# A two-layer decoder trunk on one core: the background inverses of a delta-rule layer paced among the v and gate projections, with the remainders of split numbers on VectorE

## The chip, the cores and the metric

The kernel runs on one core of a Trainium2 chip. The metric is device time in microseconds (us). The time before is the median of three runs. Engines are called as in the profile: PE is TensorE, DVE is VectorE, ACT is ScalarE, POOL is GpSimd, SP is SyncE, which here only issues transfers.

## What is computed

The input x is 1024 tokens by 1024 features. Layer 0 is a time-mixing layer with a matrix state for each of 16 heads, layer 1 a differential attention. After each, a gated input embedding (PLE) is added, and at the end stands one normalization. The change lies in layer 0, of which this is what matters:

```
dx = token_shift(h) - h
xm = h[:, :, None, :] + dx[:, :, None, :] * mu[:4]        # inputs of r, k, v and gate
proj = einsum('bsgd,dgc->bsgc', xm, w_in)                 # 1024 x 1024 each
r, k, v, gate = proj
...
def step(state, inp):                                     # over the 1024 tokens
    r_t, w_t, k_t, v_t, kk_t, b_t = inp
    sa = einsum('bhij,bhj->bhi', state, kk_t)
    state = state * w_t - sa[..., None] * b_t + v_t[..., None] * k_t
    y_t = einsum('bhij,bhj->bhi', state, r_t)
    return state, y_t
...
return (y * silu(gate)) @ w_out
```

All is 32-bit. A product of full precision is made of three matmuls: each operand is split into a rounded half (hi, on ACT) and the remainder (lo, one subtraction), and hi·hi, hi·lo, lo·hi are summed.

## The kernel before

The recurrence runs in 16 chunks of 64 tokens. For each chunk and head the steps inside the chunk need the inverse of a 64x64 triangular matrix, and these inverses depend only on k and b, not on the state. They are made ahead, as a background to two projections, in four quarters of four chunks.

One quarter goes so. For each of its four chunks PE makes products (`pb`), and DVE scales them into `nq`. DVE transposes the diagonal 32x32 blocks into `nb`. Then 31 elimination steps of two instructions each follow: `tm` is a product of one column of `nb` with a row of `tb`, and `tb` takes the sum; the operands have between 31 and 256 elements per partition. DVE transposes the result twice, into `ea` and into `ti`. The off-diagonal blocks come from two more groups of 64 small matmuls, `pg` and `po`, with ACT's copies `prhs` and `pairs` ahead of each; this is the merge. All 16 `ti` are needed before the core.

The stages in question follow the projections of k and r. The v projection (about 307 to 447 us) has 32 tiles, each with 24 matmuls of 128x256; ACT copies each tile to SBUF (`vst`) and SP stores it (`v_d`). The gate projection (447 to 565 us) has 16 blocks `d`, each with 24 matmuls of 128x512; ACT makes a tanh of it and DVE the gate (`ge`), which goes out to `sg_d`. Then comes the core: per chunk the chain of `xy`, `u` and `s` on PE, with `kbt`, `pm`, `prt` of the next chunk, and with the products `pps` of layer 1's embedding between them.

Weights come as raw rows (`wv10r`, `w_6r`, two buffers) and are split by `wload`; the inputs of the gate projection (`xm3`) are made by `make_half`: a multiply on ACT, a multiply-add on DVE, hi on ACT, lo on POOL or DVE. `split` puts remainders on POOL unless told otherwise:

```
def split(hi, lo, src, lo_eng=None):
    S.activation(hi, src, AF.Copy)
    (lo_eng or G).tensor_tensor(out=lo, in0=src, in1=hi.bitcast(F32), op=ALU.subtract)
```

The background is a generator, `inv_steps`; `tick` takes a step of it at two points of each v tile and four points of each gate block, and the work is written into the program there. Engines are in order each. Up to the core a scheduler may still move instructions within an engine's list; from the core loop on, `e.pin` keeps the order in which they are written. `first` holds the opening pieces of the core's first chunk (`stage1`: load, decayed, turn, mh, pr), which are written behind the inverses. `ple_load(1, ...)` loads and splits p and wp, the operands of `pps`, ahead of the core.

## Time and profile before

| | us |
|---|---|
| median of three runs | 1796.63 (1793.05 to 1798.04) |
| the profiled execution | 1792.27 |
| its span | 1790.4 |
| PE busy in the span | 1676.9 (94%) |
| DVE busy | 1272.1 (71%) |
| ACT busy | 798.9 (45%) |
| POOL busy | 609.0 (34%) |
| v projection, inverses in the background | about 307 to 447 |
| gate projection, inverses in the background | about 447 to 565 |
| core, 16 chunks | about 565 to 860 |

The profile shows one execution. Busy shares are means over stages with different limits. So a stage is read from its own window, then from the chain of waits, which is followed back from the last instruction, and from the rows of what each engine waited for. The table of the whole span says little about a stage.

### The profile page before, as it was taken

How to read it: one execution, taken by the hardware profiler on the slowest of the kernel's cores; microseconds unless marked ns; L12 is line 12 of the kernel's file. 1: busy time of each engine (PE TensorE's matmuls, PEld its weight loads, DVE VectorE, ACT ScalarE, POOL GpSimd, SP SyncE). 2: the span in 40 equal slices, each digit the busy share in tenths (PEclk: the TensorE clock that was granted, in tenths of full speed). 3: DMA queues.
4: the chain of work that ended last, by engine and by line, in shares of the span. 5: the costliest groups of instructions: out<-in, count | busy, mean ns of one | idle time of the engine just before them, and what ended most of it. 6: DMA issues, size and time to landing. Idle time of an engine off the chain costs nothing.

```text
span 1790.4 us, 31127 instructions
## 1 busy us (share of the span) xinstructions
PE 1676.9 (94%) x11768; PEld 1391.3 (78%) x11768; DVE 1272.1 (71%) x2910; ACT 798.9 (45%) x1690; POOL 609.0 (34%) x647
## 2 busy tenths in 40 slices
PE   6899999898998989999899899899999999999998
PEld 5677778887677878887678778788888888777786
DVE  7865845698994476666756657887787887856665
ACT  6567743346344443334434344444444444444332
POOL 4433634224323455656300342332423323311200
PEclk9999999998898999999899999999999999999999
DMA  7115444434216553453523210110111101521122
GB/s 261 53 54 165 140 121 104 131 99 117 82 62 192 168 172 119 131 167 113 212 101 135 93 60 7 53 49 17 54 33 30 56 9 55 188 70 34 59 95 71
DMA packets 164404, 176.03 MB, mean 98 GB/s; under 512 B 74845, under 2 KB 127837, under 8 KB 164254
## 3 DMA queue, kind: packets, MB, share of 16 engines
q1 hardware_dynamic: 161950, 169.84, 30.6%
q10 hardware_dynamic: 2304, 4.20, 0.6%
q8 instruction: 93, 1.52, 0.4%
q14 instruction: 57, 0.47, 0.1%
HBM read 124.19 MB, written 49.81 MB: 97 GB/s over the span
## 4 chain that ended last, share of the span: by engine, by line
PE 63%; DVE 25%; issue 4%; ACT 4%; POOL 3%; DMA 1%; SPq 0%; ACTq 0%; DVEq 0%; POOLq 0%
PE qkv L50 18%; PE d L50 7%; PE fg L50 5%; PE pg L50 5%; PE do L50 4%; PE sc L50 3%; DVE xmt L50 3%; PE xy L50 3%; PE av L50 3%; DVE tm L50 3%; PE op L50 3%; DVE tb L50 3%; DVE nb L50 2%; DVE ost L50 2%; PE pm L50 1%
## 5 line engine op out<-in xcount | busy, mean ns | idle before, releaser
L50 ACT ACTIVATE e<-sc,mx 128x256 f32<-128x256 f32 (+7 forms) x128 | 94.1, 739 | 110.7 <-DVE mx L50 59.7
L50 POOL TENSOR_TENSOR rp<-rp,rq 128x128 f32<-128x128 f32 x128 | 61.7, 503 | 227.8 <-DVE rq L50 173.8
L50 PE MATMUL sc<-k,q 128*128 128x512 f32 (+2 forms) x384 | 88.7, 363 | 3.8 <-ACT e L50 2.2
L50 PE MATMUL av<-vh,aT 128*128 128x128 f32 x576 | 81.2, 281 | 6.3 <-DVE aT L50 6.3
L50 PEld LDWEIGHTS av<-vh,aT 128*128 128x128 f32 x576 | 75.6, 195 | 12.8 <-DVE aT L50 8.9
L50 POOL TENSOR_TENSOR m<-m,mmask 128x512 f32<-128x512 f32 x32 | 47.9, 1496 | 81.7 <-ACT m L50 81.7
L50 DVE TENSOR_REDUCE mxs<-sc 128x1 f32<-128x128 f32 (+6 forms) x112 | 73.9, 680 | 0.5
L50 PEld LDWEIGHTS sc<-k,q 128*128 128x128 f32 x384 | 63.2, 190 | 12.9 <-ACT e L50 3.0
L50 PE MATMUL pg<-pwg,ph 128*128 128x512 f32 x224 | 73.2, 405 | 0.0
L50 PE MATMUL do<-dwo,oh 128*128 128x512 f32 x224 | 71.7, 401 | 0.8 <-DVE h L50 0.6
L50 DVE SCALAR_TENSOR_TENSOR xmt<-hT,cB,xmt 128x512 f32<-128x512 f32 x64 | 63.6, 1011 | 6.2 <-ACT xmt L50 5.8
L50 ACT ACTIVATE o<-av,r 128x128 f32<-128x128 f32 x64 | 23.5, 368 | 90.1 <-PE av L50 89.9
L50 DVE TENSOR_TENSOR tm<-tb,nb 128x31 f32<-128x31 f32 (+15 forms) x124 | 57.1, 461 | 3.6
L50 DVE SCALAR_TENSOR_TENSOR e<-e,r,e 128x128 f32<-128x128 f32 (+3 forms) x64 | 56.7, 887 | 1.2
L50 POOL CAST q<-q 64x128 fp32r<-64x128 f32 x128 | 38.8, 304 | 52.2 <-PE sc L50 48.0
L50 POOL CAST k<-k 64x256 fp32r<-64x256 f32 x64 | 25.7, 401 | 84.6 <-ACT k L50 83.5
L50 DVE TENSOR_TENSOR tb<-tb,tm 128x31 f32<-128x31 f32 (+15 forms) x124 | 51.8, 417 | 3.6
L50 DVE TENSOR_TENSOR rp<-qkv,rc 128x256 f32<-128x256 f32 x64 | 27.0, 421 | 36.7 <-PE qkv L50 34.0
L50 DVE COPY aT<-at 128x512 f32<-128x512 f32 (+2 forms) x96 | 51.8, 549 | 1.1 <-PE at L50 0.4
L50 PE MATMUL at<-ident,e 128*128 128x128 f32 x288 | 47.4, 277 | 3.1 <-DVE e L50 2.6
L50 DVE SCALAR_TENSOR_TENSOR ost<-ost 128x2 f32<-128x2 f32 x192 | 47.4, 247 | 3.8
L50 DVE TENSOR_TENSOR m<-pm,mmask 128x512 f32<-128x512 f32 x32 | 22.1, 691 | 38.2 <-PE pm L50 38.1
(1136 smaller groups left out, 5602.7 us busy)
## 6 DMA issues: line engine op xcount, KB each, us to landing
pp_d<-ppo SPq DMA_DIRECT2D x32, 256.0 KB, 2.5
kb_d<-kb SPq DMA_DIRECT2D x16, 512.0 KB, 3.3
kkr<-kkr_d SPq DMA_DIRECT2D x32, 256.0 KB, 3.8
kb<-kb_d SPq DMA_DIRECT2D x32, 256.0 KB, 3.5
x<-in_x SPq DMA_DIRECT2D x8, 512.0 KB, 5.8
kkr_d<-ep SPq DMA_DIRECT2D x16, 256.0 KB, 2.6
kkr_d<-rt SPq DMA_DIRECT2D x16, 256.0 KB, 2.6
bb<-kb_d SPq DMA_DIRECT2D x32, 128.0 KB, 2.9
```

The source lines that it names most:

```text
L50: r = f(*a, **k)
```

## The change

1. The inverses are one generator, `inverses`, whose yields say about how many us of DVE's time a step holds; `tick` adds us and takes steps while it is owed some. The merge of a quarter is written between the elimination steps of the next (behind steps 1, 3, 11 and 15), and the `pb` of the next quarter behind steps 19, 22, 25 and 28. `nb` is one transpose of 128 partitions and two of 32, instead of four of 32.
2. All remainders of the v and gate weights and of the `xm3` inputs are on DVE; loading and splitting stand at fixed points (`wfetch`, `wsplit`, `mixer`).
3. `e.pin` is set from the v projection on, so that the order of four engines is the written one there.
4. `vst` has a pool of its own with one buffer, where it shared three with `xmt` and `ge`.
5. The gate is one DVE instruction instead of two; its factor 0.5 goes into `split_half` in the core. Its store is issued on SP's queue instead of ACT's.
6. The opening pieces of the core (`first`) are taken between the gate's matmuls once the inverses are written. The state is set first, and p and wp are loaded behind the first `vload` and split within chunk 0 (`pw_split`).

```diff
+    def split_half(hi, lo, src):
+        S.activation(hi, src, AF.Copy, scale=0.5)
+        V.scalar_tensor_tensor(out=lo, in0=src, scalar=0.5, in1=hi.bitcast(F32), op0=ALU.mult, op1=ALU.subtract)
...
+    PACE = 1.36
...
+        vo_cm = NB("vo")
+        vo = vo_cm.__enter__()
...
+                if cc < 2:
+                    load(cc + 2)
...
+            def merge(q):
+                ti, ea = tis[q], eas[q]
+                for st, y in blocks:
+                    o = 64 * st
+                    S.copy(prhs[o + 32 * y:o + 32 * y + 32], ea[o:o + 32, 16 * y:16 * y + 16])
+                for st in range(2):
+                    r = slice(64 * st + 32, 64 * st + 64)
+                    S.copy(ti[r, :, 32:64], ti[r, :, 0:32])
+                    G.memset(ti[r, :, 0:32], 0.0)
+                yield
+                pg = products(q, "pg")
+                yield
+                for st, y in blocks:
+                    o = 64 * st
+                    r = slice(o + 32 * y, o + 32 * y + 32)
+                    S.copy(prhs[r], ti[o + 32:o + 64, 16 * y:16 * y + 16, 32:64])
                     S.copy(pairs[r, :, 32 * y:32 * y + 32], pg[st][r])
-                    S.copy(prhs[r], ti[o + 32:o + 64, hs_, 32:64])
                 yield
-            for _ in range(Y2 + 1):
+                po = products(q, "po")
...
+            nx = inv_pb(0)
+            for _ in nx:
+                yield VW
+            for q in range(4):
+                nqf, ti = nqs[q], tis[q]
+                mg = merge(q - 1) if q else iter(())
+                nb = inv4("nb", f"nb{q}")
+                V.transpose(nb, nqf[:, :, 0:32].rearrange("p h t -> p t h"))
+                yield 2.2
+                next(mg, None)
+                for st in range(2):
+                    r = slice(64 * st + 32, 64 * st + 64)
+                    V.transpose(nb[r], nqf[r, :, 32:64].rearrange("p h t -> p t h"))
+                    yield 2.0
+                tb = inv4("tb", f"tb{q}")
+                G.memset(tb, 0.0)
+                G.memset(tb.rearrange("p a b -> p (a b)")[:, 0::33], 1.0)
+                tm = iv.tile([P, 256], F32, tag="tm", name=f"tm{q}", bufs=1)
+                nx = iter(())
+                for j in range(31):
+                    w, n = j + 1, 31 - j
+                    tv = tm[:, 0:n * w].rearrange("p (n w) -> p n w", w=w)
+                    V.tensor_tensor(out=tv, in0=tb[:, j:j + 1, 0:w].to_broadcast([P, n, w]),
+                                    in1=nb[:, j + 1:32, j:j + 1].to_broadcast([P, n, w]), op=ALU.mult)
+                    V.tensor_tensor(out=tb[:, j + 1:32, 0:w], in0=tb[:, j + 1:32, 0:w], in1=tv, op=ALU.add)
+                    if j % 2:
+                        yield 1.45
+                    if j in (1, 3, 11, 15):
+                        next(mg, None)
+                    if j == 17:
+                        for st, y in blocks:
+                            o = 64 * st
+                            S.copy(pairs[o + 32 * y:o + 32 * y + 32, :, 32 * y:32 * y + 32],
+                                   nqf[o:o + 32, 16 * y:16 * y + 16, 32:64])
+                        if q < 3:
+                            nx = inv_pb(q + 1)
+                            next(nx)
+                    if j in (19, 22, 25, 28) and q < 3:
+                        next(nx)
+                        yield 0.85
+                yield 0.9
+                ea = eas[q] = inv4("ea", f"ea{q}")
+                V.transpose(ea.rearrange("p h s -> p s h"), tb.rearrange("p t s -> p s t"))
+                V.transpose(ti[:, :, 0:32].rearrange("p h t -> p t h"), tb)
+                yield 4.2
+            for _ in merge(3):
+                yield 4.0
...
-            while due[0] >= 1.0:
-                due[0] -= 1.0
-                next(bg, None)
+            while live[0] and due[0] > 0.0:
+                t = next(bg, None)
+                if t is None:
+                    live[0] = False
+                else:
+                    due[0] -= t
...
-            V.tensor_scalar(out=e, in0=e, scalar1=0.5, scalar2=0.5, op0=ALU.mult, op1=ALU.add)
-            V.tensor_tensor(out=e, in0=ps, in1=e, op=ALU.mult)
-            nc.scalar.dma_start(out=sg_d[j, :, half(hf)], in_=e)
-        new = [None, None]
+            V.scalar_tensor_tensor(out=e, in0=e, scalar=1.0, in1=ps, op0=ALU.add, op1=ALU.mult)
+            nc.sync.dma_start(out=sg_d[j, :, half(hf)], in_=e)
...
+        def wsplit():
+            if wrs:
+                nm, r = wrs.pop(0)
+                h, lo = wpair(nm)
+                split(h, lo, r, V)
+                due[0] -= 1.3
+                ws.append((h, lo))
...
+                if kt:
+                    h_, lo_, t_ = ts[-1]
+                    split(h_, lo_, t_, V)
+                    xs.append((h_, lo_))
+                if kt < KT:
+                    V.scalar_tensor_tensor(out=t, in0=hT[:, kt, half(hf)], scalar=cB[:, 3, kt:kt + 1], in1=t,
+                                           op0=ALU.mult, op1=ALU.add)
+                    due[0] -= 1.5
...
+        VW = 1.56 * PACE
+        wfetch()
+        wfetch()
+        wsplit()
+        wsplit()
+        due[0] = 0.0
+        for e in engines:
+            e.pin = True
...
+                    if kt == 4:
+                        if i == 7:
+                            wsplit()
+                        if q or i > 2:
+                            tick(VW)
+                        if mix:
+                            next(mix, None)
...
-                st = ab.tile([P, 512], F32, tag="xmt", name=f"vst{q}{i}", bufs=3)[:, 0:256]
+                st = vo.tile([P, 256], F32, tag="out", name=f"vst{q}{i}", bufs=1)
                 S.copy(st, ps)
                 nc.sync.dma_start(out=v_d[i * P:(i + 1) * P, q * 256:(q + 1) * 256], in_=st)
+                if i in (0, 4):
+                    wfetch()
+                if i == 3:
+                    wsplit()
+                    if q == 3:
+                        mix = mixer(0)
                 if q or i > 2:
-                    tick(TV)
-                if q == 3 and i % 4 == 3:
-                    new[i // 4] = make_half(3, i // 4)
+                    tick(VW)
...
-            if npt[0] < 48:
-                tick(TG)
-            elif npt[0] == 48:
-                tick(1000)
+            next(mix, None)
+            if live[0]:
+                tick(GW)
+            elif not early:
...
-                p0, p1 = pieces0 = stage1(0, 0), stage1(1, 0)
-                first.extend(pc[nm] for nm in ("load", "decayed", "turn", "mh", "pr") for pc in pieces0)
-                first.append(p1["bonus"])
+                p0, p1 = stage1(0, 0), stage1(1, 0)
+                p0["load"]()
+                p1["load"]()
+                first.extend([lambda: None, p0["decayed"], p0["mh"], p0["pr"], p0["turn"], p1["decayed"], p1["mh"],
+                              p1["pr"], p1["turn"], p1["bonus"]])
...
-        pw1 = ple_load(1, lambda nm, dt: big(*ptags.pop(0), nm, dt))
...
+        pw1, pw_raw = ([], []), []
+        for kt in range(2):
+            for x, src, nm in ((0, A["pT"], "p"), (1, A["pwp"], "wp")):
+                r = big(*ptags.pop(0), f"{nm}1{kt}", F32)
+                nc.sync.dma_start(out=r, in_=src[1, :, kt])
+                pw_raw.append((x, r, big(*ptags.pop(0), f"{nm}h1{kt}"), big(*ptags.pop(0), f"{nm}l1{kt}")))
+        def pw_split():
+            for _ in range(2):
+                x, r, h, lo = pw_raw.pop(0)
+                split(h, lo, r, G if x else V)
+                pw1[x].append((h, lo))
...
-            more()
+            if c:
+                more()
             unit("mh", 0)
+            if not c:
+                pw_split()
+                pw_split()
```

How the rows move at three places, in the lists of the two programs.

PE, from the last `pg` to the core's first `xy`, before (`d` with w_6 and w_7 are the gate's last blocks; 38 `d` stand between `pg` and `po`, 26 behind):

```order
L50 MATMUL pg_4957<-prhs,pairs 64x32
L50 MATMUL d_5284<-xm_2_0h,w_7l 128x512
...
L50 MATMUL d_5352<-xm_7_1h,w_6h 128x512
L50 MATMUL po_5024<-prhs,pairs 64x32
...
L50 MATMUL po_5023<-prhs,pairs 64x32
L50 MATMUL d_5352<-xm_7_1l,w_6h 128x512
...
L50 MATMUL d_5396<-xm_7_1h,w_7l 128x512
L50 MATMUL kbt_0_5291<-ident,kbp_0_5269 128x128 x4
L50 MATMUL kbt_0_5303<-ident,kbp_0_5282 128x128 x4
L50 MATMUL pm_0_5316<-kkr_0_5226,kb_0_5227 128x128
```

The same place after the change (36 `d` between `pg` and `po`, 54 up to the first `pm`, then three times 12):

```order
L50 MATMUL pg_5088<-prhs,pairs 64x32
L50 MATMUL d_5061<-xm_6_1h,w_4h 128x512
...
L50 MATMUL po_5185<-prhs,pairs 64x32
...
L50 MATMUL d_5177<-xm_2_0h,w_6h 128x512
...
L50 MATMUL pm_0_5311<-kkr_0_5273,kb_0_5274 128x128
...
L50 MATMUL d_5295<-xm_4_1h,w_6h 128x512
...
L50 MATMUL kbt_0_5341<-ident,kbp_0_5302 128x128 x4
...
L50 MATMUL pm_0_5363<-kkr_0_5277,kb_0_5278 128x128
...
L50 MATMUL kbt_0_5392<-ident,kbp_0_5354 128x128 x4
L50 MATMUL prt_0_5398<-rk_5269,pr_0_5329 64x2 x8
L50 MATMUL xy_5467<-state,kkr_0_5273 128x64 x8
```

Behind the last `pg` stand 126 rows of `d` instead of 64, and the core's pieces stand between them.

ACT at the start of the v projection, before (`xm_4_1h` and the like are the v projection's inputs; three copies `vst` follow):

```order
L50 ACTIVATE wv10h<-wv10r 128x1024
L50 ACTIVATE xm_4_1h<-xmt_4_1_2639 128x512
...
L50 ACTIVATE xm_7_1h<-xmt_7_1_2660 128x512
L50 COPY vst_2714<-v_2689 128x256
L50 COPY vst_2742<-v_2717 128x256
L50 COPY vst_2770<-v_2745 128x256
```

After:

```order
L50 COPY vst_2717<-v_2692 128x256
...
L50 ACTIVATE xm_7_1h<-xmt_7_1_2660 128x512
L50 COPY vst_2747<-v_2722 128x256
L50 COPY vst_2775<-v_2750 128x256
L50 COPY vst_2819<-v_2778 128x256
L50 ACTIVATE wv10h<-wv10r 128x1024
L50 COPY vst_2903<-v_2852 128x256
```

`wv10h` moved behind the copies of four tiles. On DVE its remainder `wv10l` now stands right ahead of the first scaling `nq`, where the remainder of `xm_7_1` stood before; in all 11 remainders of weights (wv11 to w_5), 16 of `xm3` and 10 `ge` stand between the first `nq` and the last `ti`.

SP's queue at the end of the gate projection, before (`kkr` and `kb` are the core's operands):

```order
L166 DMA kkr_1_5480<-kkr_d 128x4x128
L130 DMA p_5441<-in_pT 128x1024
L130 DMA wp_5447<-in_pwp 128x1024
L130 DMA p_5453<-in_pT 128x1024
L130 DMA wp_5459<-in_pwp 128x1024
L874 DMA vu_5470<-v_d 64x512 x2
L1063 DMA lnw<-in_lnw 128x1024
L168 DMA kb_1_5477<-kb_d 128x4x128
L874 DMA vu_5488<-v_d 64x512 x2
L963 DMA rwo0r<-in_rwo 128x1024
L963 DMA rwo1r<-in_rwo 128x1024
L168 DMA kb_1_5481<-kb_d 128x4x128
```

After:

```order
L694 DMA sg_d<-ge_5337 128x512
L173 DMA kb_1_5457<-kb_d 128x4x128
L694 DMA sg_d<-ge_5388 128x512
L980 DMA vu_5430<-v_d 64x512 x2
L1172 DMA p_5433<-in_pT 128x1024
L1172 DMA wp_5437<-in_pwp 128x1024
L1172 DMA p_5441<-in_pT 128x1024
L1172 DMA wp_5445<-in_pwp 128x1024
L1182 DMA lnw<-in_lnw 128x1024
```

The loads of p and wp moved behind the gate's last store and chunk 0's `vu`.

## Rows read from the trace of the kernel before

**Rows 1.** Windows of the trace: us, then busy PE, PEld, DVE, ACT, POOL; PEclk.

```profile
307.00:447.00 140.00, 125.56 (x1463) 119.70 (x1462) 114.99 (x188) 65.69 (x114) 45.80 (x30) 0.93 0.43 115
...
324.57:543.00 218.43, 202.04 (x1856) 175.06 (x1855) 191.25 (x346) 96.52 (x161) 60.49 (x39) 0.91 0.35 99
543.00:564.70 21.70, 20.93 (x194) 17.21 (x195) 4.51 (x9) 11.48 (x19) 4.98 (x8) 0.92 0.54 170
```

**Rows 2.** Chain of waits from 324 to 565 us, shares by line.

```profile
by line: DVE tm L50 23.0%; DVE tb L50 20.7%; DVE nb L50 12.5%; PE d L50 7.0%; issue 5.5%; PE v L50 4.8%; DVE ge L50 4.3%; DVE ea L50 3.7%; DVE xmt L50 3.3%; DVE nq L50 3.1%; ACT prhs L50 2.8%; DVE ti L50 1.5%; ACT xmt L50 1.2%; PE pb L50 1.
```

**Rows 3.** What PE waited for, 307 to 575 us: total, times, longest.

```profile
PE pb L50 <- DVE nq L50: 5.6, 2, 3.1
PE pg L50 <- ACT prhs L50: 5.0, 3, 3.1
```

**Rows 4.** Chain of waits from 543 to 600 us: start, us, what.

```profile
543.77 2.06 PE pg L50 x64
545.83 10.61 PE d L50 x38
...
558.42 6.27 PE d L50 x26
...
575.42 5.51 PE xy L50 x64
580.94 2.86 PE pps L50 x6
...
596.39 3.01 PE xy L50 x64
```

**Rows 5.** The page's costliest groups: tm and tb.

```profile
L50 DVE TENSOR_TENSOR tm<-tb,nb 128x31 f32<-128x31 f32 (+15 forms) x124 | 57.1, 461 | 3.6
...
L50 DVE TENSOR_TENSOR tb<-tb,tm 128x31 f32<-128x31 f32 (+15 forms) x124 | 51.8, 417 | 3.6
```

**Rows 6.** Views of tiles tb, xmt, rwo2l: ns min/median/max, first and last start.

```profile
L50 DVE TENSOR_TENSOR tm<-tb,nb x124: 192/360/2518, 347.6 to 538.5; 128x31 f32<-128x31 f32 x8, 128x60 f32<-128x60 f32 x8, 128x87 f32<-128x87 f32 x8, 128x112 f32<-128x112 f32 x8
...
L50 DVE SCALAR_TENSOR_TENSOR xmt<-hT,cB,xmt x64: 699/744/2772, 44.0 to 467.3; 128x512 f32<-128x512 f32 x64
...
L50 ACT ACTIVATE xm_1h<-xmt x32: 612/630/636, 75.4 to 468.1; 128x512 fp32r<-128x512 f32 x32
...
L50 DVE TENSOR_TENSOR xm_1l<-xmt,xm_1h x11: 625/682/1657, 76.8 to 456.4; 128x512 fp32r<-128x512 f32 x11
...
L50 DVE TENSOR_TENSOR rwo2l<-rwo2r,rwo2h x1: 1225/1225/1225, 649.6 to 649.6; 128x1024 fp32r<-128x1024 f32 x1
```

**Rows 7.** Timelines of POOL and DVE at 518 us: start, us, instruction.

```profile
517.92 2.37 POOL L50 TENSOR_TENSOR w_6l<-w_6r,w_6h 128x1024 fp32r<-128x1024 f32 x1 [9.11 <-ACT w_6h L50]
...
518.04 2.52 DVE L50 TENSOR_TENSOR tm<-tb,nb 128x252 f32<-128x252 f32 x1
```

**Rows 8.** DVE's groups, 324.57 to 543: busy, mean ns, idle before.

```profile
L50 DVE STREAM_TRANSPOSE nb<-nq 32x1024 f32<-32x1024 f32 x16 | 32.2, 2010 | 0.2
L50 DVE SCALAR_TENSOR_TENSOR xmt<-hT,cB,xmt 128x512 f32<-128x512 f32 x16 | 13.7, 869 | 5.6 <-ACT xmt L50 5.6
L50 DVE TENSOR_TENSOR nq<-pb,rn 128x256 f32<-128x256 f32 x32 | 12.2, 418 | 11.7 <-PE pb L50 11.7
L50 DVE STREAM_TRANSPOSE ea<-tb 128x1024 f32<-128x1024 f32 x4 | 8.9, 2213 | 0.1
L50 DVE STREAM_TRANSPOSE ti<-tb 128x1024 f32<-128x1024 f32 x4 | 7.9, 1972 | 0.0
...
L50 DVE TENSOR_TENSOR ge<-d,ge 128x512 f32<-128x512 f32 x11 | 7.5, 681 | 0.0
```

**Rows 9.** Timeline of ACT at the start of the v stage.

```profile
326.12 0.37 ACT L50 COPY vst<-v 128x256 f32<-128x256 f32 x1 [0.73 <-DMA v_d<-vst]
```

**Rows 10.** DMA issues, 300 to 570 us: KB each, median us to landing.

```profile
v_d<-vst SPq DMA_DIRECT2D x32, 128.0 KB, 2.1
...
wp<-in_pwp SPq DMA_DIRECT2D x2, 512.0 KB, 10.3
```

More of the change, by code (lines that the diff above doesn't have):

```diff
@@ L540, in inv_pb, with load @@
             nqs[q] = nq.rearrange("p c h j l -> p (c h j) l")
-            for cc in range(4):
+            ops = []
+            def load(cc):
                 c = 4 * q + cc
@@ L611, in inv_merge, with inverses, products @@
-        def inv_merge(q):
-            for _ in range(Y1):
-                yield
-            ti = tis[q]
-            prhs, pairs = ivt
-            def products(nm):
+                yield
+        def inverses():
+            prhs, pairs = ivt[:] = (iv.tile([P, 16, 32], F32, name="prhs"), iv.tile([P, 16, L], F32, name="pairs"))
+            G.memset(pairs, 0.0)
+            blocks = [(st, y) for st in range(2) for y in range(2)]
+            eas = {}
+            def products(q, nm):
                 pg = [pp.tile([P, 16, 32], F32, tag="tr", name=f"{nm}{q}{st}", bufs=2) for st in range(2)]
@@ L644, in inv_merge @@
                 yield
-        def inv_steps():
-            for q in range(5):
-                def first():
-                    if q < 4:
-                        yield from inv_pb(q)
-                        yield from inv_diag(q)
-                a, b = first(), inv_merge(q - 1) if q else iter(())
-                alive = True
-                while alive:
-                    alive = False
-                    for g in (a, b):
-                        if next(g, g) is not g:
-                            alive = True
-                            yield
@@ new lines, in trunk, with wfetch @@
+        wsrc += [(f"w3_{j}", A["wT"][2][j]) for j in range(KT)]
+        wrs, ws = [], []
+        def wfetch():
+            if wsrc:
+                nm, src = wsrc.pop(0)
+                r = wraw(nm + "r")
+                nc.sync.dma_start(out=r, in_=src.rearrange("p k c -> p (k c)"))
+                wrs.append((nm, r))
+        def wsplit():
[5 more added lines that the diff above has]
+                ws.append((h, lo))
@@ L681, in trunk @@
+        new = [[], []]
+        mix = None
+        VW = 1.56 * PACE
[6 more added lines that the diff above has]
+            e.pin = True
         for q in range(4):
-            wv = [wload(f"wv{q}{k2}", A["wv"][q, k2].rearrange("p k c -> p (k c)")) for k2 in range(2)]
+            wv = ws[2 * q:2 * q + 2]
             for i in range(NT):
@@ L1089, in tile_ @@
             return TP[i]
-        for e in engines:
-            e.pin = True
         for c in range(NCH):
```

115 lines of the change are left out of this document (54 added, 61 removed).

## The prediction

> **What bounds the kernel now.** I read the busy shares by stretch first, then the chain of waits, then what PE and DVE waited for, then the costs of DVE's operations, then the order of the two programs. From the first inverse product to the last transpose of the inverses DVE is busy for 191.25 of 218.43 us [rows 1], and in the chain of the v and gate stages DVE's elimination steps (tm 23.0%, tb 20.7%), its transposes nb (12.5%) and its smaller work hold far more than PE's d and v (7.0% and 4.8%) [rows 2]. PE shows 202 us busy there, but its waits are where it reads what DVE makes: pb behind nq, pg behind the copies of ea [rows 3]. So up to the last ti the time is set by DVE, and the end of the gate stage is that moment plus what PE still has to do behind the last pg. That tail is in the chain: pg 2.06, 38 d up to 556.44, po up to 558.42, 26 d [rows 4]. Then chunk 0 of the core follows, up to chunk 1's xy at 596.39.
>
> I cut the change at three moments of the profiled execution: first nq 324.57, last ti over at 543.00 (the window's bound [rows 1]), last d over at 564.69 (558.42 + 6.27 [rows 4]).
>
> **1. DVE's own work between first nq and last ti.**
> - tm and tb, 248 of them: busy 57.1 + 51.8 = 108.9 us [rows 5], though the median tm takes 0.360 and the longest 2.518 [rows 6]. The long ones lie beside a remainder on POOL: a tm of 252 columns took 2.52 while POOL's w_6l ran for 2.37 [rows 7]. After the change POOL makes no remainder here. Priced at 0.36 and 0.02 to the next: 248 × 0.38 = 94.
> - nb: 16 of 2.01 are 32.2 now [rows 8]. After: 8 of them at 2.01 and 4 of 128 partitions, priced as ea (2.21): 25.
> - ea and ti: 4 × (2.21 + 1.97) = 16.7, unchanged [rows 8].
> - nq: 32 in 12.2, unchanged [rows 8].
> - The 16 xm3 inputs: 16 × 0.744 for the multiply-add as now (median [rows 6]), and all 16 remainders, of which 14 are new, at 0.682 [rows 6]: 22.8. Their present multiply-adds took 13.7 [rows 8].
> - Weights' remainders: the order puts 11 (wv11 to w5) between first nq and last ti; a 128x1024 one took 1.225 on DVE [rows 6]: 13.5. New.
> - ge: 10 of one operation instead of 11 to 12 of two, at the 0.681 of the one that reads d [rows 8]: 6.8.
> Sum 191.0, against 191.25 busy before. What leaves DVE (collisions 15, nb 7, the first operation of each ge) comes back as remainders (11 of the weights', 14 of the inputs').
>
> By the Trainium skill ("SBUF — State Buffer", section "Who interferes with whom") a DVE instruction with two SBUF inputs and a GpSimd one that reads SBUF shut each other out, and the second blocks for the first's whole length. The trace agrees, 2.52 beside 2.37 [rows 7]. By that rule alone the change takes some 20 us from DVE; by the sum it takes none, since the work is moved onto DVE, not removed.
>
> **2. DVE's waits there.** Now 218.43 - 191.25 = 27: 11.7 on pb, 5.6 on ACT's first half of an input [rows 8], the rest mostly on tanh. After: three pb of a quarter's four stand between elimination steps, so PE can make the next while DVE works; I leave 6 for the first quarter, where nothing stands between. Each xm3 remainder comes right behind ACT's rounding of 0.63 [rows 6]: 16 × 0.5 = 8. Sum 14, so **13 less**. Bounds: none left (27 less), all left (0 less).
>
> **3. The start.** The store tile of v has one buffer where three were shared. A copy now waits until the store before it has landed: 0.37 [rows 9], an issue (estimate 0.4) and 2.1 [rows 10], 2.9 together. In the new order three such copies stand on ACT ahead of wv10h, and wv10l on DVE ahead of the first nq: 2 × 2.9 behind the first copy, then twice 0.63 for a rounding of double width, then 1.225. That is 8.3, less the 1.26 of wv10h that stood ahead of the copies before, less some 3 that the multiply-adds of this place lost to POOL (median 0.744, longest 2.772 [rows 6]): **4 later**. Bounds 0 and 8. Later a v tile comes every 140/32 = 4.4 us (307 to 447, [rows 1]), more than 2.9, so the single buffer costs nothing there; if tiles came at PE's bare rate, it would be the limit.
>
> The Trainium skill ("Trainium Kernel Development and Optimization", section "Best Practices") asks for double buffers, so that transfers overlap with work, and so speaks against the one buffer. The trace bears it out at the start alone, where the wait on a store was 0.73 with three buffers [rows 9]; by the rule every tile would wait, by the sum three do.
>
> **4. The tail behind the last pg.** Before, 64 d stand there, now 126 (front section, PE's order), because the inverses are asked for earlier per piece of PE work. 126 × 0.241 (6.27/26, full clock [rows 4]) = 30.4; pg and po 4.0; 16 pm and eight kbt of a quarter of a d's columns, 24 × 0.06 = 1.4; after the wait the first 38 d took 10.61 instead of 9.16 [rows 4], 1.5; from ti's end to pg 0.8 as now (543.77). Sum 38.1, against 21.7 (543.00 to 564.69): **16 later**. The early pm and kbt are hidden in nothing, they are PE's time in both, only their waits on other engines are covered.
>
> Last d: +4 - 13 + 16 = **7 later**, near 572.
>
> **5. From last d to chunk 1's xy.** Before 31.7 us, 16.25 to pps (580.94) and 15.45 from it to xy (596.39) [rows 4]. Now chunk 0's pieces (kbt, pm, m, prt) lie between the gate's matmuls, so xy follows the last d at once; it started 10.7 behind it (575.42 [rows 4]), and that alone would give up to 10. But the store of the last ge is on SP's queue now, and behind it stand vu0, then p and wp. They issue some 4 us after the last d (tanh, ge, five issues: estimate), wp takes 10.3 to land [rows 10], where it was there before; rounding and remainder of 128x1024 take 1.26 + 1.225 at least, so pps starts near 17 to 18. The 1.4 of pm and kbt and their waits no longer stand behind it: 12 to 14 to xy. Sum 31: **1 earlier**, 5 earlier to 3 later.
>
> **6. The rest.** 16 gl in the core read two operands as before (0.682 class), ±0. The issue of 16 stores moves from ACT to SP, both with idle time. The later stages have the same orders but for a few rows: ±2.
>
> **Sum:** 1792.27 + 7 - 1 = 1798.3 for an execution like the profiled one. That one lies 4.4 below the median of 1796.63, so the forecast is **1803** (1798.3 + 4.4), some 6 above.
>
> **Rivals.**
> - **DVE's waits vanish (faster).** Products, merges and remainders spread over the steps could leave DVE without a pause, and the remainders of xm3 may find ACT done long before. Then -27 + 4 + 16 = -7 at the last d, with the start at +2 and the core's boundary at -4: about -13, 1784. It decides from the point where the 27 us of waits fall under 6. For it: the pauses now come in lumps (pb 11.7 in all). Against: each remainder directly follows a rounding on ACT, whose queue also holds the copies of vst.
> - **The two cancel (same).** Waits fall to 7 instead of 14 and the start costs 2: -20 + 2 + 16 - 1 = -3, so 1794 to 1799.
> - **Waits stay (far slower).** A single buffer, a fixed order and ACT's copies put every late store in front of what DVE needs; the waits remain 27 and the start costs 8: +8 + 16 = +24, near 1820. For it: nothing can overtake in the fixed order. Against: 4.4 us per tile against 2.9.
> - **The order isn't kept:** excluded, since the built program has the rows in this order.
>
> **Numbers.** A measurement of this kernel can tell about 0.3% (5.4 us) from no change: faster is below 1791.2, slower above 1802.0. My forecast stands only just on the slow side; the wide term is DVE's waits. Forecast and small neighbours 0.40, waits stay 0.10, so slower 0.50; cancelled 0.23; waits vanish 0.27. The range reaches into both rivals, 1783 to 1816, and leaves out the end of each, about 2 in 10. The forecast's own range is 1797 to 1810.
>
> **What would show it.** Right: no remainder on POOL between 330 and 540, tm and tb at 0.42 at most, DVE's busy time near 191, first nq near 328, last ti near 534, pg at 535, last d near 572, pps some 17 behind it, xy of chunk 1 near 602. Wrong: last ti before 525 (waits vanish), or after 543 (they stay); long tm without POOL, which would mean another cause for them; If the last d is where I say and the total isn't, the step on the core's boundary failed.

## Result and the profile after

The changed kernel took 1806.28 us (median of five runs, 1802.59 to 1809.35), the kernel before 1794.84 in runs beside it (five, 1793.05 to 1798.04). The ratio is 1.0057 with a 95% interval of 1.0037 to 1.0077: slower, by about 10 us (the medians differ by 11.4). The forecast was 1803, slower by 6 us or so. The profiled execution of the changed kernel took 1808.91 with a span of 1807.1, so it lies 2.6 above its median, where that of before lay 4.4 below its own. One of the five runs of the kernel without a fixed order (under Experiments) took 2702.78 us at a granted clock of 0.573 and stands in no ratio; the median of its other four is 1779.7.

The first view is the windows between the moments at which the prediction cut the change: first `nq`, last `ti` over, last `d` over (columns as in [rows 1]).

```profile
329.70:534.90 205.20, 181.56 (x1782) 157.56 (x1782) 174.08 (x354) 92.62 (x155) 9.05 (x12) 0.91 0.35 97
534.90:576.80 41.90, 41.24 (x296) 33.59 (x298) 7.62 (x10) 16.86 (x26) 8.98 (x12) 0.88 0.27 85
576.80:607.30 30.50, 22.07 (x265) 18.30 (x264) 9.71 (x10) 10.60 (x19) 15.00 (x11) 0.83 0.84 259
```

DVE's stretch is 205.2 us long against 218.43 [rows 1], with 174.08 busy against 191.25. The tail behind it is 41.9 (to 576.8) against 21.7.

The chain of waits of the changed kernel at the end of the gate projection (start, us, what) answers to [rows 4]:

```profile
535.56 3.63 PE pg L50 x64
539.19 11.13 PE d L50 x36
550.33 1.99 PE po L50 x64
...
552.31 12.70 PE d L50 x54
...
573.41 2.96 PE d L50 x12
...
577.37 0.81 PE xy L50 x11
578.17 3.08 DMA vu<-v_d
...
588.65 1.90 POOL wpl L50
...
591.26 3.33 POOL wpl L50
...
594.63 1.22 PE pps L50 x2
...
607.27 3.01 PE xy L50 x64
```

The tail is there as foretold: 36, 54 and three times 12 `d` behind `pg`. But `pg` took 3.63 where it took 2.06, and the first 36 `d` took 11.13, 0.31 each, where 54 later ones took 12.70, 0.235 each. PE had stood for 4.1 us before `pg`, and the windows show what clock it was granted then (columns as above, the clock is the third number from the end):

```profile
535.50:539.20 3.70, 3.64 (x65) 3.58 (x65) 0.00 (x0) 2.09 (x3) 1.89 (x2) 0.50 0.21 75
539.20:545.00 5.80, 5.80 (x14) 4.57 (x15) 1.89 (x2) 2.86 (x5) 0.00 (x0) 0.52 0.12 45
545.00:550.40 5.40, 5.40 (x29) 4.09 (x27) 0.71 (x2) 4.89 (x8) 0.00 (x0) 1.00 0.00 0
```

That is the lower of its two levels, 1.2 of 2.4 GHz, up to some 545 us, and the full one behind it. Behind the last `d` (573.41 + 2.96 = 576.37) stand four kbt and 16 prt, xy starts at 577.3 and waits 3.08 for vu. The first six `pps` are the next waits of PE (timeline):

```profile
588.62 0.50 PE L50 MATMUL pps<-wph,ph 128*128 128x512 f32 x1 [0.91 <-ACT wph L50]
591.35 0.50 PE L50 MATMUL pps<-wpl,ph 128*128 128x512 f32 x1 [2.23 <-POOL wpl L50]
...
594.63 0.79 PE L50 MATMUL pps<-wpl,ph 128*128 128x512 f32 x1 [2.32 <-POOL wpl L50]
```

The first starts 12.2 us behind the last `d`; two of them wait for POOL's remainders of wp, and the six are over at 595.85, 7.2 us after the start of the first, where the six took 2.86 before [rows 4].

What PE and DVE waited for in DVE's stretch (total, times, longest) answers to [rows 3, 8]:

```profile
PE pb L50 <- DVE nq L50: 22.2, 4, 7.5
...
PE pg L50 <- ACT prhs L50: 4.3, 2, 4.1
```

```profile
DVE nq L50 <- PE pb L50: 6.7, 4, 3.2
...
DVE xm_1l L50 <- ACT xm_1h L50: 4.5, 7, 0.7
DVE xm_0l L50 <- ACT xm_0h L50: 3.5, 5, 0.7
DVE wv31l L50 <- ACT wv31h L50: 2.4, 1, 2.4
DVE wv21l L50 <- ACT wv21h L50: 2.1, 1, 2.1
DVE ge L50 <- ACT ge L50: 2.0, 2, 1.1
DVE tm L50 <- POOL tb L50: 1.3, 2, 0.9
```

The waits of PE at `pb` grew from 5.6 to 22.2. DVE's wait of 11.7 for `pb` fell to 6.7, but waits behind ACT's roundings of weights and inputs took its place.

The view of the tile tb and the costs by shape show the collisions gone: the longest tm took 2.518 [rows 6] and takes 0.426, and one of 252 columns, which took 2.52 beside w_6l [rows 7], takes 422 ns on the mean of eight.

```profile
L50 DVE TENSOR_TENSOR tm<-tb,nb x124: 184/360/426, 346.6 to 530.5; 128x31 f32<-128x31 f32 x8, 128x60 f32<-128x60 f32 x8, 128x87 f32<-128x87 f32 x8, 128x112 f32<-128x112 f32 x8
...
L50 DVE TENSOR_TENSOR tm<-tb,nb 128x252 f32<-128x252 f32 x8 | 3.4, 422 | 0.3
```

The start of the v projection on ACT and DVE (timeline: start, us, instruction, and in brackets the wait ahead of it) answers to [rows 9]:

```profile
325.00 0.37 ACT L50 COPY vst<-v 128x256 f32<-128x256 f32 x1 [1.93 <-DMA v_d<-vst]
327.24 0.37 ACT L50 COPY vst<-v 128x256 f32<-128x256 f32 x1 [1.87 <-DMA v_d<-vst]
327.50 1.06 ACT L50 ACTIVATE wv10h<-wv10r 128x1024 fp32r<-128x1024 f32 x1
...
328.60 1.23 DVE L50 TENSOR_TENSOR wv10l<-wv10r,wv10h 128x1024 fp32r<-128x1024 f32 x1 [5.06 <-ACT wv10h L50]
329.74 0.75 DVE L50 TENSOR_TENSOR nq<-pb,rn 128x256 f32<-128x256 f32 x2
```

Two copies wait 1.93 and 1.87 for the store before them, `wv10h` comes behind them, and DVE stands 5.06 us until it is there. The first `nq` is at 329.74, 5.2 later than before. Of these 5.2 the first matmul of v already shows 1.7 (308.96 against 307.23), ahead of the copies; counted from it the first `nq` is 3.4 later.

### The profile page after: what moved, and what is told of

It reads as the page before. It is cut to its first block, busy times and chain, and to the rows that moved or that the text cites. A ratio compares the mean times of both kernels' runs of the same rounds, so it can differ in the third digit from the quotient of the medians.

```text
span 1807.1 us, 31104 instructions
## 1 busy us (share of the span) xinstructions
PE 1679.8 (93%) x11768; PEld 1392.8 (77%) x11768; DVE 1255.3 (69%) x2920; ACT 799.9 (44%) x1690; POOL 549.0 (30%) x617
## 3 DMA queue, kind: packets, MB, share of 16 engines
q1 hardware_dynamic: 164254, 174.03, 30.9%
## 4 chain that ended last, share of the span: by engine, by line
PE 65%; DVE 19%; ACT 4%; issue 4%; POOL 4%; DMA 3%; SPq 1%; ACTq 0%; POOLq 0%; DVEq 0%
PE qkv L50 18%; PE d L50 8%; PE fg L50 5%; PE pg L50 5%; PE do L50 4%; PE sc L50 4%; PE av L50 3%; DVE xmt L50 3%; PE op L50 3%; PE xy L50 3%; DVE tm L50 2%; DVE tb L50 2%; PE pm L50 2%; DVE ost L50 1%; PE at L50 1%
## 5 line engine op out<-in xcount | busy, mean ns | idle before, releaser
L50 POOL MEMSET ti<- 32x1024 f32 x8 | 7.6, 946 | 203.8 <-ACT ti L50 132.3
L50 DVE SCALAR_TENSOR_TENSOR xmt<-hT,cB,xmt 128x512 f32<-128x512 f32 x64 | 59.9, 951 | 0.5 <-ACT xmt L50 0.2
L50 PEld LDWEIGHTS pg<-pwg,ph 128*128 128x128 f32 x224 | 42.0, 192 | 9.6 <-ACT ph L50 0.5
```

The source lines that it names most:

```text
L50: r = f(*a, **k)
```

## Experiments

Each is one or two edits of one of the two kernels, timed beside runs of the kernel before. Ratios are to those runs, whose medians lie between 1794.84 and 1796.54; the changed kernel stands at 1.0057. The moments are those of one profiled execution each. The two kernels with shared buffers and a fixed order have the same rows in the same order up to the core, and their moments differ by 1.9 at the first nq (and already at the first matmul of v, 307.91 and 305.99) and by 4.2 at last ti and last d. So a difference of some 4 us between two executions shows nothing by itself.

| kernel | median us | ratio (interval) | first nq | last ti over | last d over | xy of chunk 1 |
|---|---|---|---|---|---|---|
| before | 1794.84 | 1 | 324.6 | 543.0 | 564.7 | 596.4 |
| the change | 1806.28 | 1.0057 (1.0037 to 1.0077) | 329.7 | 534.9 | 576.4 | 607.3 |
| weights' remainders on POOL | 1815.57 | 1.0108 (1.0084 to 1.0132) | 323.0 | 543.2 | 583.4 | 613.4 |
| shared buffers for v's stores | 1803.83 | 1.0031 (1.0015 to 1.0048) | 325.3 | 530.8 | 572.0 | 603.0 |
| PACE 1.28 | 1808.58 | 1.0066 (1.0043 to 1.0089) | 329.5 | 543.6 | 566.8 | 607.5 |
| gate's stores on ACT's queue | 1822.02 | 1.0136 (1.0110 to 1.0162) | 327.8 | 546.2 | 589.9 | 621.4 |
| no fixed order before the core | 1779.83 | 0.9895 (0.9868 to 0.9922) | 325.6 | 522.8 | 542.7 | 580.3 |
| before, remainders on DVE | 1781.01 | 0.9912 (0.9889 to 0.9935) | 322.5 | 533.1 | 542.6 | 581.2 |
| shared buffers, core's start | 1804.61 | 1.0045 (1.0028 to 1.0062) | 323.4 | 526.6 | 567.8 | 602.1 |
| PE alone free | 1810.59 | 1.0069 (1.0052 to 1.0087) | 329.4 | 541.8 | 575.8 | 610.3 |
| DVE alone free | 1815.27 | 1.0097 (1.0077 to 1.0117) | 322.7 | 543.1 | 583.5 | 615.7 |
| PE and DVE free | 1794.92 | 0.9987 (0.9970 to 1.0003) | 322.6 | 528.3 | 562.0 | 596.1 |
| no fixed order, shared buffers | 1772.31 | 0.9862 (0.9839 to 0.9884) | 323.1 | 522.6 | 542.7 | 575.7 |
| the same, p and wp loaded early | 1776.35 | 0.9882 (0.9862 to 0.9902) | 322.3 | 520.7 | 540.7 | 572.7 |

### The weights' remainders back on POOL

```diff
-                split(h, lo, r, V)
+                split(h, lo, r, G)
```

> The changed kernel with one thing undone: the 16 remainders of the v and gate weights go back to POOL, in the same written order. Theory A (the remainders cost DVE about what the collisions cost it before): DVE loses 11 x 1.22 = 13.4 us of work, and gets collisions back, which before were 108.9 - 79 = 30 us in tm and tb for some 24 remainders on POOL, 1.25 each, so 11 x 1.25 = 14. Last ti within 5 of the changed kernel's 534.9, the whole within 5 of it. Theory B (the remainders on DVE are the loss): last ti 13 earlier, the whole 10 to 13 us faster than the changed kernel. Theory C (the collisions are worse, since in the fixed order nothing can step aside): last ti 8 or more later.

Last ti came at 543.2, 8.3 later than in the changed kernel, though the first nq came 6.7 earlier, and the whole took some 9 us more. That is theory C. DVE's stretch is 220.2 us long with 175.22 busy:

```profile
323.00:543.20 220.20, 182.64 (x1782) 158.63 (x1782) 175.22 (x343) 94.08 (x157) 39.45 (x26) 0.91 0.33 92
```

The tiles view has the long ones again:

```profile
L50 DVE TENSOR_TENSOR tm<-tb,nb x124: 183/360/2642, 348.0 to 538.9; 128x31 f32<-128x31 f32 x8, 128x60 f32<-128x60 f32 x8, 128x87 f32<-128x87 f32 x8, 128x112 f32<-128x112 f32 x8
```

Busy time grew by 1 us where 13.4 of work had left, so the collisions cost 14, as theory A had it; what it missed is that 14 us of waits came on top. In the waits DVE stands 11.7 us at tm for POOL's clearing of tb, and 14.2 us at nq for pb. The first of the three clearings follows the remainder wv11l on POOL; the other two follow the clearing of ti, which waits for ACT's copies. In the changed kernel DVE waits 1.3 for POOL's clearings in all:

```profile
DVE nq L50 <- PE pb L50: 14.2, 4, 7.3
DVE tm L50 <- POOL tb L50: 11.7, 3, 4.0
```

So the weights' remainders on DVE, taken alone, are a gain of the change, not its loss.

### Three shared buffers for v's stores

```diff
-                st = vo.tile([P, 256], F32, tag="out", name=f"vst{q}{i}", bufs=1)
+                st = ab.tile([P, 512], F32, tag="xmt", name=f"vst{q}{i}", bufs=3)[:, 0:256]
```

> The changed kernel with the store tile of v back on the three buffers that it shared with the inputs and gates. Theory A: the copies at the start no longer wait for a store each (1.9 us twice), wv10h comes 4 us earlier and the first nq at 325 to 326 instead of 329.7; all behind it moves by as much, so the whole is 3 to 4 us faster. Rival: the inputs of the gate now wait for v's stores, and what is won at the start is lost later; then last ti stays within 1 of 534.9.

First nq at 325.3, 4.4 earlier, and all behind it moved by as much: last ti by 4.1, last d by 4.4, chunk 1's xy by 4.3. The medians differ by 2.5 us, and the intervals of the two ratios overlap. Counted from the first matmul of v, the first nq comes at 17.4 instead of 20.8 us, 3.4 earlier, and the other kernel with shared buffers in this order shows the same 17.4. So the single buffer costs some 3 us at the start. Later in the v projection ACT waits for a store five more times in the changed kernel (378 to 421 us, 11.9 in all, the longest 4.56), but the stretch from first nq to last ti is 205.2 us with one buffer and 205.3 with three.

### A slower pace

```diff
-    PACE = 1.36
+    PACE = 1.28
```

> The changed kernel with PACE 1.28 instead of 1.36. Only the written order moves: 78 d stand behind the last pg instead of 126, 42 of them behind po, and the core's opening pieces stand behind all d. Theory A (the tail is PE's work that was left over while it waited for DVE): the last d comes 48 x 0.235 = 11 us earlier, if DVE's end does not move; from there to chunk 1's xy it takes 30 to 36 us, since the loads behind the last store take as long as the pieces; the whole is 6 to 11 us faster, near the kernel before. Rival: DVE now waits for PE's products, last ti comes 8 or more later, and the whole is not faster.

The tail did shrink: last d at 566.8, 9.6 earlier. But last ti came at 543.6, 8.7 later, which I had given to the rival, and chunk 1's xy came at 607.5, where it was. From last d to that xy it now took 40.7 us instead of 30.9, beyond the 36 that I had allowed. The whole did not gain. So fewer d in the tail did not make this kernel faster: DVE's end came later, and the d that cover the core's opening pieces are not all lost time.

### The gate's stores on ACT's queue

```diff
-            nc.sync.dma_start(out=sg_d[j, :, half(hf)], in_=e)
+            nc.scalar.dma_start(out=sg_d[j, :, half(hf)], in_=e)
```

> The changed kernel with the gate's stores issued on ACT's queue, as before, instead of SP's. Theory A: the loads of chunk 0's vu, p and wp no longer stand behind the last gate on SP; they are issued some 8 us or more earlier, xy no longer waits 3 us for vu nor pps some 4 us for POOL's remainder of wp, and from the last d to chunk 1's xy it takes 24 to 27 us instead of 30.5; the last d stays within 2 of 576.8; the whole is 4 to 6 us faster. Rival: ACT stands still at each issue until DVE has made the gate, which comes late in the fixed order; then the copies for pg and po are late too, and the last d comes 3 or more later, which takes back the gain.

Theory A fell, and the rival cost far more than I had put on it: last d came 13.5 later, and the whole took 16 us more. From last d to chunk 1's xy it was 31.5, no shorter at all. ACT's waits show what the rival foretold (total, times, longest):

```profile
ACT ge L50 <- DVE tm L50: 5.7, 1, 5.7
ACT prhs L50 <- DVE tb L50: 3.7, 1, 3.7
ACT prhs L50 <- DVE ge L50: 3.3, 1, 3.3
```

ACT stands at the issue of a store until DVE has made the gate, and prhs, the next tanh and the next rounding wait behind it. In the fixed order the move of these stores to SP is worth 16 us.

### The order not fixed before the core

```diff
-        for e in engines:
-            e.pin = True
         for q in range(4):
             wv = ws[2 * q:2 * q + 2]
...
+        for e in engines:
+            e.pin = True
         for c in range(NCH):
```

> The changed kernel with the engines' written order kept from the core loop on only, as before, instead of from the v projection on; the scheduler may then move rows, and 50 d stand behind the last pg in its list, with the core's opening pieces behind all of them. Theory A (DVE's sum sets last ti, whatever the list): last ti stays within 5 of the changed kernel's 534.9, the last d comes at 553 to 560, the pieces are uncovered and chunk 1's xy follows 35 to 41 us later, at 590 to 600; the whole is 8 to 16 us faster than the changed kernel, equal to the kernel before. Theory B (the written order is what keeps DVE's waits short, as the run with PACE 1.28 suggests): last ti 8 us or more later, and the whole not more than 4 us faster.

1779.83, 26 us less than the changed kernel and 16 less than the kernel before, more than either theory allowed. Last ti came 12.1 earlier, where theory A had it within 5 and theory B later: the order of the lists does move it. 4.1 of the 12.1 are the start (counted from the first matmul of v the first nq is at 17.1 us instead of 20.8, although the single buffer is still there) and 8.0 the stretch. Last d came 33.7 earlier, and chunk 1's xy 27.0 earlier, since the core's opening pieces then stood uncovered (37.6 us from last d). The same stretch of DVE and the two waits between PE and DVE:

```profile
325.60:522.80 197.20, 186.81 (x1831) 162.43 (x1832) 172.55 (x355) 94.34 (x156) 9.03 (x12) 0.97 0.38 104
```

```profile
PE pb L50 <- DVE nq L50: 2.7, 2, 2.1
...
DVE nq L50 <- PE pb L50: 12.9, 5, 5.7
```

DVE's busy time is the same (172.55 against 174.08). Its idle time is 24.6 instead of 31.1, PE's wait for nq is 2.7 instead of 22.2, and the granted clock of PE in the stretch is 0.97 instead of 0.91.

### The kernel before with the remainders on DVE

```diff
-            split(h, lo, r)
+            split(h, lo, r, V if nm[:2] == 'wv' or nm[:3] == 'w3_' else G)
...
-            split(h, lo, t, V if kt % (2 if g == 1 else 3 if g != 3 else 8) == 1 else G)
+            split(h, lo, t, V if g == 3 or kt % (2 if g == 1 else 3) == 1 else G)
```

> The kernel before with one part of the change: the remainders of the v and gate weights and of the gate's inputs are on DVE instead of POOL. Theory A (the remainders on DVE gain, as undoing them lost): DVE loses 30 us of collisions in tm and tb and gets 12 x 1.22 + 14 x 0.69 = 24 us of work; with the waits as before last ti comes 5 to 8 earlier than 543.0 and the whole is 4 to 8 us faster than the kernel before. Theory B (the gain in the changed kernel needs its written order; here the scheduler puts remainders where DVE or PE waits for them): no change or up to 10 us slower.

14 us less than the kernel before, near twice what theory A allowed. Its stretch from first nq to last ti:

```profile
322.50:533.10 210.60, 197.18 (x1869) 171.70 (x1868) 188.31 (x377) 97.53 (x161) 9.19 (x12) 0.95 0.37 105
```

210.6 us with 188.31 busy, so DVE has only 2.9 us less work, 4.9 less waiting, and the stretch also begins 2.1 earlier. Behind the last pg stand 16 `d` instead of 64, since the scheduler put the others ahead of it, so the tail from last ti to last d (542.6) is 9.5 us instead of 21.7. From last d to chunk 1's xy it is 38.5 instead of 31.7. So of the 22 us by which last d comes earlier, 2 are the start, 3 DVE's work, 5 its waits and 12 the tail, where the scheduler, which was given other rows, made another list; 7 are lost again behind last d. Part 2 of the change, alone and in the old order, gains more than the whole change loses, but little of that is DVE's work.

### The core's start

```diff
-                nc.sync.dma_start(out=r, in_=src[1, :, kt])
+                nc.scalar.dma_start(out=r, in_=src[1, :, kt])
...
-                split(h, lo, r, G if x else V)
+                split(h, lo, r, V)
```

> The changed kernel with v's stores on the three shared buffers, as in the run before, and two edits at the core's start: p and wp are loaded on ACT's queue, where nothing waits, and their four remainders are all on DVE instead of two on POOL. Theory A (the late loads behind the last gate's store, and POOL's 5.9 us for the remainders of wp, set the time from last d to chunk 1's xy): pps starts 4 us earlier, and it takes 26 to 28 us from last d to chunk 1's xy instead of 30.5 to 31; the whole is 3 to 5 us faster than with the shared buffers alone. Rival: chunk 0's chain itself (vu0, x, u, s) is what bounds; then the stretch stays within 1 us of 30.5.

The kernel has the shared buffers too. Last d came at 567.8 and chunk 1's xy at 602.1, so the stretch is 34.3 us, longer than 30.9, and the whole is the same as with shared buffers alone. Both accounts missed; the first pps starts 17.4 us behind the last d instead of 12.6 with shared buffers alone. The chain shows transfers in the place of POOL:

```profile
570.36 8.18 DMA vu<-v_d
...
578.99 6.50 DMA kkr<-kkr_d
...
585.53 0.56 DVE wpl L50
...
589.92 1.22 PE pps L50 x2
```

vu0's second load needs 8.18 us to land, where in the changed kernel its two loads took 3.42 and 3.10, and the next chunk's kkr 6.50. Here p and wp, 512 KB each, were issued on ACT's queue 0.7 and 0.3 us ahead of vu0's 128 KB; in the changed kernel they follow it on SP's. So having the big loads first made the small one late that xy needs (PE waits 7.89 us for it).

### One engine free, or two

```diff
         for e in engines:
-            e.pin = True
+            e.pin = e is not T
```

(and `e is not V`, `e not in (T, V)` for the other two; from the core loop on all are fixed)

> The changed kernel with PE alone left to the scheduler up to the core loop; DVE, ACT and POOL keep the written order. Only PE's rows move: products pb stand 22 to 28 matmuls apart instead of 12, and 96 d stand behind the last pg instead of 126. Theory A (the loss of the fixed order is PE standing 22 us at products whose space in PSUM DVE has not yet read, with work for which it had time written behind them): these waits fall under 6 us, the last d comes 12 to 20 us earlier than 576.4, the whole is 12 to 20 us faster than the changed kernel. Theory B (DVE's and ACT's fixed order holds the chain): last ti stays at 535 and the whole gains no more than the 30 d that left the tail, 7 us.

> The changed kernel with DVE alone left to the scheduler up to the core loop; PE, ACT and POOL keep the written order. Only DVE's rows move. Theory A of the run with PE alone: PE's waits stay at 18 to 24 us, and the whole is within 4 us of the changed kernel. Theory B: DVE's waits behind ACT's roundings (8 us at the remainders of the gate's inputs, 10 at those of weights) fall under 4, last ti comes 8 us or more earlier, and the whole is 8 us or more faster.

> The changed kernel with PE and DVE both left to the scheduler up to the core loop; ACT and POOL keep the written order. Theory A (PE's and DVE's lists must be arranged together: free alone, each only trades its own waits for the other's): the sum of PE's and DVE's waits at pb and nq falls under 20 us (29 in the changed kernel, 30 with PE alone free), and most of the 26 us that freeing all engines gained comes back, 14 us or more. Theory B (ACT's written order holds the chain, its copies of v and its roundings standing in a row that waits for PE): last ti stays at 534 or later and the whole is not more than 6 us faster than the changed kernel.

With PE alone free, PE's wait at pb fell to 7.1 us, but DVE's at nq rose to 22.7, last ti came 6.9 later, and the whole was not faster than the changed kernel. With DVE alone free, the waits behind the inputs' remainders went away as theory B had it, and PE's wait for nq at pb fell to 7.8 us with DVE's at nq at 10.8. But last ti came 8.3 later, with new waits (DVE for ACT's tanh 7.4, for ACT's copies 5.1 and for POOL's clearing 5.1; PE 7.7 for loads of kk and 10.5 for remainders of the v weights), and the whole was 9 us slower. So all four theories of these two runs fell. With both free the sum of the two waits is 11.5 us and the whole is 11 us faster than the changed kernel, equal to the kernel before: theory A in its mechanism, less than the 14 it asked for; 26 come with all four engines free. The waits at pb and nq, first PE alone free, then both:

```profile
DVE nq L50 <- PE pb L50: 22.7, 8, 5.5
...
PE pb L50 <- DVE nq L50: 7.1, 2, 4.8
```

```profile
DVE nq L50 <- PE pb L50: 9.5, 2, 4.9
...
PE pb L50 <- DVE nq L50: 2.0, 1, 2.0
```

So freeing PE's list or DVE's list alone does not help: the first moves the wait at pb to DVE's nq, the second brings waits of other kinds. The last step, from 1794.92 to 1779.83, comes when ACT and POOL are free too; then wv10h, wv20h and wv30h each stand four copies of v earlier in ACT's list, and PE's and DVE's lists are others again. ACT alone and POOL alone were not freed, so it is not shown whether the order of one of them is enough, and which rows matter is open.

### The best of them

> The changed kernel with the scheduler left free up to the core loop and v's stores on the three shared buffers. If both losses add, it is 3 to 4 us faster than with the scheduler free alone, near 1776. If the scheduler already hides the one buffer, it is within 2 us of 1780.

> As the run before, and p and wp are loaded and split ahead of the core again, as in the kernel before, instead of behind chunk 0's vu. Theory A (from last d to chunk 1's xy the late loads set the time, 37.6 us with the scheduler free against 31.7 before): the stretch is 31 to 33 us, and the whole 4 to 6 us faster than the run before, near 1771. Rival: chunk 0's own chain bounds, since now no d covers the pieces; then within 2 us of the run before.

```diff
-        pw1, pw_raw = ([], []), []
...
+        pw1 = ple_load(1, lambda nm, dt: big(*ptags.pop(0), nm, dt))
         co_cm = NB("core")
...
-            if c:
-                more()
+            more()
```

No fixed order and shared buffers together took 1772.31, 1.4% less than the kernel before and 7.5 us less than without the shared buffers (the intervals overlap). But in the profiles last ti (522.6 and 522.8) and last d (542.7 both) stay where they were; chunk 1's xy is 4.6 earlier because it follows last d in 33.0 us instead of 37.5. So that the two losses add is not shown: up to last d the free order hides the single buffer, as the second account had it, and why the core's start is shorter is open. With p and wp loaded ahead of the core, as before the change, the stretch from last d to chunk 1's xy is 31.9 us, within what theory A asked for, but it had started from 33.0 and not from 37.6. PE no longer waits at pps, and waits 4.62 us for vu0, which is now issued behind p and wp and takes 8.81 and 8.60 us to land. The median was 4 us more, where theory A had it 4 to 6 less; the intervals overlap, and where these us went behind chunk 1's xy is open. Four versions beat both kernels: the kernel before with its remainders on DVE, and the three with no fixed order before the core. The fastest is the one with shared buffers and late loads.

## Why the prediction came out right

**The direction came out, and so did most of the sum, but in two places by errors that cancel.** By its steps:

- *DVE's own work* was put at 191.0 and was 174.08. The sum priced tm and tb at the median of one tm, 0.36, and 0.02; the mean over the 16 shapes is 0.342, and both together took 42.3 + 42.6 = 84.9 us where I had 94 with the gaps (costs of the changed kernel by line, 307 to 560 us):

```profile
L50 DVE TENSOR_TENSOR tb<-tb,tm 128x31 f32<-128x31 f32 (+15 forms) x124 | 42.6, 343 | 4.3
L50 DVE TENSOR_TENSOR tm<-tb,nb 128x31 f32<-128x31 f32 (+15 forms) x124 | 42.3, 341 | 4.6 <-POOL tb L50 1.3
```

  So the collisions had cost 108.9 - 84.9 = 24 us, not 15. The other terms were nb 24.2 for 25, nq 12.0 for 12.2, inputs 11.9 + 11.0 for 22.8, ge 6.8 for 6.8, and a weight's remainder 1.22 for 1.225. With 11 of these and 16.6 for ea and ti the terms sum to some 181; the busy time is 7 less, since it counts once what two instructions share at their ends. So the step that the work stays the same failed: 17 us of it went.
- *Its waits* were put at 14 and were 31.1. The two that I had counted were right (6.7 for 6, and 8.0 for 8); missed were the roundings wv21h and wv31h that stand behind copies of v on ACT (4.5), ge (2.0), POOL's clearing of tb, and the small gaps, which the sum had put into the price of tm and tb. DVE was to wait 13 less than before and waited 4 more (31.1 for 27.2). This error and the last have the same size and opposite signs, so the stretch came out at 205.2, as summed (205), 13 shorter for another reason than the one given. That much agreement is luck.
- *The start* was 5.2 later for 4, with the two waits on a store that the step described; counted from the first matmul of v it is 3.4, and shared buffers give that back. That the single buffer makes no wait later, at 4.4 us a tile, did not hold: ACT waited for a store five more times. It cost nothing in the stretch.
- *The tail* was 41.5 (534.9 to 576.37) for 38.1: 126 d as counted, but pg and the first 36 d, up to 545 us at the lower clock, cost 3.63 + 11.13 where I had put 2.0 + 10.2 or so, and 32 pm and four kbt took 2.6 us where the sum had 1.4 for half as many pm.
- *From last d to chunk 1's xy* 30.9 for 31, again by two errors that cancel: pps started 12.2 us behind the last d for 17 to 18, since wp landed in 6.1 us (median) and not in 10.3 and the first pps needs no remainder, and from there to xy it took 18.6 for 12 to 14. What the step had not seen is that PE waits twice within the first pps for POOL's remainders of wp, 4.5 us. The runs on the core's start and with early p and wp show that loads put ahead of vu0 make vu0 late.
- *The rest* was put at 0 with 2 either way; behind chunk 1's xy this execution took 1199.8 against 1194.0. Some 2 of the 6 lie at the core's end (from the last u to the last op 57.9 instead of 55.8 us), where a wait of PE for pl, 2.5 us, is new; runs of the same kernel differ by as much as the remainder.

So the profiled execution should have come out at 1798.3 and was 1808.91: 10 us over, of which the start and the tail are 5, the rest 6. The forecast of 1803 for the median was nearer, because this execution lay above its median and that of before below its own.

**What the prediction didn't see** is how much the written order costs. It took that order as given, and it put the move of the gate's stores to SP at nothing. The runs show that the parts of the change have effects of both signs that are much larger than its sum: remainders on DVE -14 in the old order, stores of the gate on SP -16 in the new one, the single buffer some 3 at the start, and the fixed order +26. With the order free the same code takes 1779.83, below the 1784 of the rival that DVE's waits vanish, but not by that mechanism: DVE is still idle for 24.6 us of its 197.2. What vanishes are PE's waits at pb (22.2 to 2.7). They are not the whole cause, since with PE alone free they fell to 7.1 and nothing was gained. PE is then busy for 186.81 of 197.2 us at a clock of 0.97, instead of 181.56 of 205.2 at 0.91, so that it does more of the gate in DVE's stretch and leaves a tail of 19.9 us (522.8 to 542.7) instead of 41.5. The prediction had counted the tail and not asked why so much was left in it.

**The rule on collisions.** The Trainium skill ("SBUF — State Buffer", section "Who interferes with whom") says that an instruction of DVE with two SBUF inputs and one of GpSimd that reads SBUF shut each other out. The runs agree: in the changed kernel, without remainders on POOL, no tm took over 0.426, and with the weights' back on POOL the longest took 2.642. The prediction said that what collisions cost comes back as work. In the old order it does, almost: with the remainders on DVE its busy time is 188.31 us against 191.25, and the 14 us gained come from the start, the waits and the tail more than from its work. In the changed kernel, where nb and ge are cheaper as well, it is 174.08.

## What to carry to other kernels

Fixing the order of four engines by hand cost 26 us here, and freeing PE or DVE alone gave none of it back. So try such a change with the order left free before judging its parts, and free engines together as well as one by one. Before moving a store's issue to an engine, look at what stands behind it on that engine while the store's data is still being made. A moment read from one execution carries a few us of noise: count it from a mark that the change cannot have moved. A sum over one engine's instructions should use the mean of each shape from the costs by shape, not the median of a mixed group, and its waits deserve the same care as its work.

## What was unexpected of the hardware

The two loads of 128 KB for chunk 0 took 2.81 and 2.75 us to land before the change, when p and wp, 512 KB for each load, were there already, and 3.42 and 3.10 after it, issued ahead of these loads on the same queue. Issued behind them they took 6.96 and 8.18 in the run on the core's start (p and wp on ACT's queue, 0.7 and 0.3 us ahead) and 8.81 and 8.60 in the run with early p and wp (same queue). And a wait shows twice: PE stood 4.1 us before pg, and then ran pg at 3.63 instead of 2.06 us and 36 matmuls of d at 0.31 instead of 0.235, some 4 us more, at a granted clock of 0.50 to 0.52 up to some 545 us. Before the change pg ran at 1.00 and the first d behind it, from 545.8 to 550 us, at 0.59.
